# Weight matrices laid out by the host in contiguous 1 MB blocks: a two-layer diffusion backbone on one core

## The chip, the cores and the metric

The kernel runs on one core of a Trainium2 chip. The metric is device time in microseconds of the whole program, inputs in HBM to output in HBM; work of the host before the launch is outside it. A core has a matrix engine (TensorE, in the profile PE for matmuls and PEld for the weight loads that run beside them), VectorE (DVE), ScalarE (ACT), GpSimd (POOL), and SyncE (SP), which here issues every DMA. The transfers are carried out by 16 DMA engines. SBUF is the on-chip memory of 128 partitions, PSUM the memory into which TensorE writes.

## What is computed

Two layers over 512 latent tokens and 256 context tokens of width 1024, all in float32. Layer 0 mixes tokens by pooling, layer 1 by attention with 8 query and 2 key/value heads; each is followed by an MLP of width 4096 with a squared ReLU. Shift, scale and gate of every sub-layer come from a linear map of the conditioning vectors (`w_ada`).

```python
for i in range(DEPTH):
    sh1, sc1, gt1, sh2, sc2, gt2 = ada_mods(c, w_ada[i], b_ada[i])
    csh1, csc1, cgt1, csh2, csc2, cgt2 = ada_mods(c_ctx, w_ada[i], b_ada[i])
    h_lat = modulate(rms_norm(x, g_mix_pre[i]), sh1, sc1)
    h_ctx = modulate(rms_norm(ctx, g_mix_pre[i]), csh1, csc1)
    if i % N_MIXERS == 0:
        y_lat = pool_mixer(h_lat, w_pool[j], pool_scale[j])
        y_ctx = None if last else pool_mixer(h_ctx, w_pool[j], pool_scale[j])
    else:
        y_lat, y_ctx = attention_mixer(h_lat, h_ctx, w_qkv[j], g_q[j], g_k[j], w_o[j], not last)
    x = x + gt1 * rms_norm(y_lat, g_mix_post[i])
    m_lat = sq_relu_mlp(modulate(rms_norm(x, g_mlp_pre[i]), sh2, sc2), w_mlp_in[i], w_mlp_out[i])
    x = x + gt2 * rms_norm(m_lat, g_mlp_post[i])
    if not last:
        ...
```

## The kernel before

**Numbers.** A float32 operand of the large matmuls is split into a high part in float32r and the rest, and a product is made as three matmuls (high by high, high by low, low by high). The splits of the weights are done on the chip, from a raw tile: ScalarE casts the high part (line 126), VectorE subtracts (line 129).

**Loads.** Every weight comes by `raw_load` (line 104): one DMA from SP into a tile `raw` of 128 partitions by 2048 floats, 1 MB. What a partition receives is several rows of the matrix, one per k, cut to the width of the piece: 8 rows of 256 floats (1 KB each) for `w_mlp_in`, `w_pool` and most of `w_ada`; 4 rows of 512 floats (2 KB) for `w_qkv`, `w_o` and the wide pieces of `w_ada` (`w` = 4 in `ada_mm`); 2 rows of 1024 floats (4 KB) for `w_mlp_out`. There are 123 such loads: 48 of `w_ada` (12 with 2 KB rows), 32 of `w_mlp_in`, 32 of `w_mlp_out`, 6 of `w_qkv`, 4 of `w_o`, 1 of `w_pool`. Raw tiles rotate through a pool of four (`rawe`, the start alone) and one of three (`rawp`); a load waits on SP until the former user of its buffer is done, and the loads behind it in SP's program wait with it.

**Stages.** Times are those of the profiled execution. *Start, 0 to 105 us:* the tokens come in and are normalised (lines 325 to 332); the conditioning maps of layer 0 are computed on TensorE, one piece at a time (`ada_mm`, line 225: matmuls of a raw tile with the conditioning columns `cond` into PSUM tile `psada`; VectorE transposes the result, line 227; `ada_sel`, line 232, brings it into columns; VectorE adds the bias into `mods`, line 243). Pooling means are matmuls with a band matrix (line 420, PSUM tile `psm`), and `centred` (lines 452 to 456) modulates them as soon as shift and scale are there. The pooling weights are scaled (line 469) and split, the pooling matmuls (line 480, `pspool`) follow, then norms, gates and the modulation for the MLP (lines 378 to 395). The order of this stage is a table of due times (`Steps`), by which the instructions are written in the program; each engine works off its own list in that order. *First MLP, 105 to about 590 us:* sixteen groups of 256 hidden units, with products of quarter matrices (`weights_sums`, lines 635 to 663; `Seven`, line 677) and output matmuls (line 773, `pso`). VectorE computes the remaining conditioning maps beside it (`ada_sum`, lines 257 to 273). *Projection and attention, about 620 to 860 us* (lines 1020, 1195 to 1237), with `w_qkv` and `w_o` in 2 KB rows. *Second MLP, from about 860 us* (lines 553 and 877), to the output.

Of the kernel before, what the change touches and what calls it, by code (L numbers as in the profile page):

```python
# [17 lines left out]
P = 128  # L18
D = 1024
# [7 lines left out]
NG = FF // 256  # L27
# [5 lines left out]
BW = P + 2 * HALO  # L33
SEGS = ((0, LAT), (LAT, CTX))
SH1, SC1, GT1, SH2, SC2, GT2 = range(6)


TC_OPTS = dict(schedule_with_timeline_sim=True)
# [15 lines left out]
def backbone(ctx: ExitStack, tc, x, c, ctx_in, c_ctx, w_ada, b_ada, g_mix_pre, g_mix_post,  # L54
# [3 lines left out]
    sy, ve, sc, gp, te = nc.sync, nc.vector, nc.scalar, nc.gpsimd, nc.tensor  # L58
# [3 lines left out]
    rawp = ctx.enter_context(tc.tile_pool(name="rawp", bufs=3, side="right"))  # L62
# [17 lines left out]
    cols = const.tile([P, 128], F32, name="cols")  # L80
# [21 lines left out]
    hL = ra[:, KT * TOK:].rearrange("p (k n) -> p k n", n=TOK)  # L102
    accv = acc.rearrange("p (t n) -> p t n", n=D)

    def raw_load(src, width, pool=None):
        t = (pool or pools[0]).tile([P, 2048], F32, tag="raw", name="raw")
        d = sy.dma_start(t.rearrange("p (a b) -> p a b", b=width), src)
        if pinned[0]:
            tc.keep_in_program_order(d)
        return t  # L110
# [24 lines left out]
    class Ring:  # L135
# [1 line left out]
            self.slots, self.n, self.halves = slots, 0, halves  # L137

        def load(self, src, width, pin=False, wait=None):
            raw = raw_load(src, width, rawp)  # L140
# [73 lines left out]
    rowsd, parts, seeded, stale = {}, {}, {}, [0]  # L214

    def ada_mm(i, m, j, w=2):
        src = w_ada[i, :, m * D + j * 256: m * D + j * 256 + w * P].rearrange("(k p) n -> p k n", p=P)
        ps = psB.tile([P, 512], F32, tag="b", name="psada")
        kn = 2048 // (w * P)
        for z in range(KT // kn):  # L220
            raw = raw_load(src[:, kn * z:kn * z + kn], w * P).rearrange("p (k n) -> p k n", n=w * P)
            for k in range(kn):
                at = kn * z + k
                q = 32 * (at % 4)
                te.matmul(ps[q:q + 32, 0:w * P], cond[:, at, :], raw[:, k, :], start=(at < 4), stop=(at >= 4))  # L225
        rows = raw[:, 0, :] if w > 2 else small.tile([P, 256], F32, tag="rows", name="rows", bufs=3)
        ve.transpose(rows, ps[:, 0:w * P])
        rowsd[i, m, j] = ps, rows, w
# [26 lines left out]
                                    op0=ALU.add, op1=ALU.mult)  # L255

    def ada_sum(i, m, j, nc_, part):
        raw = raw_load(w_ada[i, :, m * D + j * 256: m * D + (j + 1) * 256]
                       .rearrange("(k p) n -> p k n", p=P), 256).rearrange("p (k n) -> p k n", n=256)
        rows = []  # L260
        for c in range(nc_):
            r = small.tile([P, 256], F32, tag="rows", name="rows", bufs=3)
            z = ve.tensor_scalar(out=r, in0=raw[:, 0, :], scalar1=cond[:, 0, c:c + 1], scalar2=None, op0=ALU.mult)
# [198 lines left out]
    pw = []  # L462

    def pool_weights():
        wraw = raw_load(w_pool[0].rearrange("g (k p) n -> p (g k) n", p=P), 256)
        pscale = rawp.tile([P, 2048], F32, tag="raw", name="pscale")[:, 0:D]
        sy.dma_start(pscale, pool_scale[0].partition_broadcast(P))
        w4 = wraw.rearrange("p (g k n) -> p g k n", k=2, n=256)
        ve.tensor_tensor(out=w4, in0=w4, in1=pscale.rearrange("p (g n) -> p g n", n=256).unsqueeze(2)
                         .broadcast_to([P, 4, 2, 256]), op=ALU.mult)  # L470
        pw.append((wraw, wpH, wpL))
# [161 lines left out]
            put(3, j, a11, a21, ALU.subtract)  # L633

    def weights_sums(g):
        raw = raw_load(w_mlp_in[0, :, g * 256:(g + 1) * 256].rearrange("(k p) n -> p k n", p=P), 256)
        rv = raw.rearrange("p (k h n) -> p h k n", h=2, n=P)
        b11, b12, b21, b22 = (rv[:, h, 4 * u:4 * u + 4] for u in range(2) for h in range(2))
        k4 = lambda z: z.rearrange("p (k n) -> p k n", n=P)
# [77 lines left out]
    landing = ((21, SC1, 0, 4), (26.3, SH1, 0, 4), (29, SC1, 2, 2), (32, SH1, 2, 2), (39, SC1, 3, 2), (42, SH1, 3, 2),  # L717
               (47.3, GT1, 0, 4), (52.6, GT1, 2, 4), (61, SC2, 0, 4), (66, SH2, 0, 4),
               (69, SC2, 2, 2), (72, SH2, 2, 2), (74.8, SC2, 3, 2), (77.7, SH2, 3, 2))
    for z, m, j, w in landing:  # L720
# [15 lines left out]
    for n, t in enumerate(order):  # L736
        b = 55 + 3 * n
# [88 lines left out]
    def mlp1(inner, last):  # L826
# [5 lines left out]
        pool = closing.enter_context(tc.tile_pool(name="pairs", bufs=1, side="right"))  # L832
# [25 lines left out]
            return w  # L858

        def rows_of(g):  # L860
            r = raw_load(w_mlp_out[1, g * 256:(g + 1) * 256, :].rearrange("(k p) n -> p k n", p=P), D)
            r = h2(r)
            return r[:, :, 0:512], r[:, :, 512:1024]

# [58 lines left out]
        wo_ = []  # L923
        for q in range(2):
            hi, lo = whole(2 * q)
            raw = raw_load(w_mlp_out[1, (NG - 2 + q) * 256:(NG - 1 + q) * 256, :].rearrange("(k p) n -> p k n", p=P), D)
# [243 lines left out]
    aring = Ring([ra[:, 8192:12288], unit[0], unit[1], unit[2]])  # L1170

    def wo_unit(ch, kk, wait=None):
        return aring.load(w_o[0, 512 * kk:512 * kk + 512, 512 * ch:512 * ch + 512]
                          .rearrange("(k p) n -> p k n", p=P), 512, True, wait)

    steps = [(h, t) for h in range(NQ) for t in range(NL)]
    smx = {}
# [163 lines left out]
        "w_pool", "pool_scale", "w_qkv", "g_q", "g_k", "w_o", "w_mlp_in", "w_mlp_out"]  # L1341


def _rope_tables():
    half = HD // 2
    t = np.arange(LAT)
# [45 lines left out]
```

## Time and profile before

| | us |
|---|---|
| three runs | 1179.66, 1181.38, 1181.9 |
| median of the runs | 1181.38 |
| profiled execution, span from first to last instruction | 1177.7 |
| median less span | 3.7 |
| TensorE matmul busy in the span | 1142.0 |
| VectorE, ScalarE, GpSimd busy | 941.6, 638.0, 67.4 |
| moved by DMA | 147.84 MB |

The profile is of one execution; of this execution it gives the span, and no separate time. TensorE's matmuls are pipelined, so that its busy time is an upper reading. An "idle before" in brackets behind a row of the timeline names what ended the engine's wait. For DMA, the share is the mean busy share of the 16 engines, which can read some per cent over 1 when packets overlap, and "to landing" is from the issue on SP to the last byte.

### The profile page before, as it was taken

To read this page: it belongs to the slowest core of one execution; us is meant where nothing else is said; L and a number is where in the kernel's file an instruction comes from. 1 tells how busy PE (TensorE), PEld (TensorE's weight loads), DVE (VectorE), ACT (ScalarE), POOL (GpSimd) and SP (SyncE) were. 2 spreads that over 40 slices of the span, in tenths; PEclk is the share of its full clock that TensorE was granted. 3 is DMA by queue.
4 is the path that set the end of the run, shared out by engine and by line. 5 is a ranking of instruction groups with operands and counts; after the bars stand their busy time and mean duration, and the time that the engine had idled before them with its cause. 6 is when DMAs were issued, how large, how long until landed. Compare 5 with 4: busy or idle time off the path is not lost.

```text
span 1177.7 us, 15984 instructions
## 1 busy us (share of the span) xinstructions
PE 1142.0 (97%) x6170; PEld 988.8 (84%) x6170; DVE 941.6 (80%) x1546; ACT 638.0 (54%) x1087; POOL 67.4 (6%) x120
## 2 busy tenths in 40 slices
PE   5899999999999999999999999999899999999997
PEld 4579888989889988998887889998888888888886
DVE  3786778998988999896787689887686779778876
ACT  3766654555354445555676377862676446435522
POOL 2030000000000000000141210001100000000001
PEclk9899999999999999999999999999999999999999
DMA  9994223444444344344422100115334124314312
GB/s 335 353 310 183 72 72 107 143 143 144 143 143 143 116 136 143 107 133 153 180 72 77 68 1 36 37 42 186 122 116 162 67 94 143 107 36 144 107 39 104
DMA packets 100010, 147.84 MB, mean 126 GB/s; under 512 B 2736, under 2 KB 75872, under 8 KB 99936
## 3 DMA queue, kind: packets, MB, share of 16 engines
q1 hardware_dynamic: 99936, 146.84, 36.6%
q8 instruction: 48, 0.79, 0.3%
q14 instruction: 26, 0.21, 0.1%
HBM read 139.49 MB, written 7.34 MB: 125 GB/s over the span
## 4 chain that ended last, share of the span: by engine, by line
PE 52%; issue 33%; DVE 6%; ACT 4%; POOL 3%; DMA 2%; SPq 0%; POOLq 0%; DVEq 0%; ACTq 0%
PE pso L773 22%; PE psin L677 18%; PE psin L553 3%; PE po L1234 2%; PE psq L1020 2%; PE pss L1195 2%; POOL rs L169 1%; PE psada L225 1%; PE psm L420 1%; POOL rs L1029 1%; ACT junk L154 1%; DVE sm L1199 1%; PE pspt L1220 1%; DVE rows L268 1%; DVE units L1223 1%
## 5 line engine op out<-in xcount | busy, mean ns | idle before, releaser
L773 PE MATMUL pso<-units,rb 128*128 128x512 f32 x1152 | 278.9, 392 | 0.0
L773 PEld LDWEIGHTS pso<-units,rb 128*128 128x128 f32 x1152 | 214.7, 188 | 41.1
L268 DVE SCALAR_TENSOR_TENSOR rows<-raw,cond,rows 128x256 f32<-128x256 f32 x280 | 127.3, 480 | 2.0
L785 DVE TENSOR_TENSOR acc<-acc,pso 128x512 f32<-128x512 f32 x129 | 85.4, 677 | 39.4 <-PE pso L773 39.3
L553 PE MATMUL psin<-ra,rb 128*128 128x512 f32 (+1 forms) x432 | 104.8, 342 | 2.4 <-ACT ra L363 1.6
L877 PE MATMUL pso<-units,pairs 128*128 128x512 f32 x336 | 82.3, 389 | 0.0
L553 PEld LDWEIGHTS psin<-ra,rb 128*128 128x128 f32 x432 | 70.3, 189 | 13.6 <-ACT ra L363 1.9
L553 PE MATMUL psin<-ra 128*128 128x512 f32 x256 | 80.4, 389 | 0.0
L877 PEld LDWEIGHTS pso<-units,pairs 128*128 128x128 f32 x336 | 63.1, 188 | 13.1
L881 DVE TENSOR_TENSOR acc<-acc,pso 128x512 f32<-128x512 f32 x72 | 48.7, 683 | 26.4 <-PE pso L877 26.4
L167 POOL TENSOR_SCALAR ms<-ss 128x1 f32<-128x1 f32 x20 | 9.6, 482 | 1000.2 <-ACT junk L154 988.4
L677 PE MATMUL psin<-ra,units 128*128 128x384 f32 x336 | 65.5, 337 | 0.4 <-ACT psin L689 0.4
L677 PE MATMUL psin<-sums,units 128*128 128x384 f32 x336 | 64.0, 336 | 0.0
L677 PEld LDWEIGHTS psin<-ra,units 128*128 128x128 f32 x336 | 59.8, 188 | 3.9 <-ACT psin L689 0.5
L129 DVE TENSOR_TENSOR units<-raw,units 128x1024 fp32r<-128x1024 f32 (+2 forms) x49 | 55.2, 1154 | 6.5 <-ACT units L126 6.3
L677 PEld LDWEIGHTS psin<-sums,units 128*128 128x128 f32 x336 | 58.9, 188 | 1.6
L126 ACT CAST units<-raw 128x1024 fp32r<-128x1024 f32 (+2 forms) x49 | 46.9, 995 | 17.7 <-PE pso L773 13.7
L553 PEld LDWEIGHTS psin<-ra 128*128 128x128 f32 x256 | 48.1, 188 | 10.0
L553 PE MATMUL psin<-rb 128*128 128x512 f32 (+1 forms) x144 | 52.8, 367 | 0.2 <-DVE rb L364 0.2
L1020 PE MATMUL psq<-units,ra 128*128 128x512 f32 x216 | 51.7, 392 | 0.0
L783 ACT COPY acc<-pso 128x512 f32<-128x512 f32 x48 | 27.1, 586 | 43.6 <-PE pso L773 42.9
L553 PE MATMUL psin<-rb,ra 128*128 128x512 f32 x128 | 49.8, 389 | 0.0
(255 smaller groups left out, 2356.0 us busy)
## 6 DMA issues: line engine op xcount, KB each, us to landing
raw<-in_w_ada SPq DMA_DIRECT2D x48, 1024.0 KB, 5.4
raw<-in_w_mlp_in SPq DMA_DIRECT2D x32, 1024.0 KB, 5.4
raw<-in_w_mlp_out SPq DMA_DIRECT2D x32, 1024.0 KB, 5.1
raw<-in_w_qkv SPq DMA_DIRECT2D x6, 1024.0 KB, 5.2
spill<-xr SPq DMA_DIRECT2D x10, 512.0 KB, 9.1
xr<-spill SPq DMA_DIRECT2D x10, 512.0 KB, 6.6
raw<-in_w_o SPq DMA_DIRECT2D x4, 1024.0 KB, 4.9
xr<-in_x SPq DMA_DIRECT2D x4, 512.0 KB, 4.2
```

Of the source, the lines that this page charges most:

```text
L126: a = sc.copy(hi, raw)
L129: b = ve.tensor_tensor(out=lo, in0=raw, in1=hi, op=ALU.subtract)
L268: ve.scalar_tensor_tensor(out=r, in0=raw[:, k, :], scalar=cond[:, k, c:c + 1], in1=r, op0=ALU.mult, op1=ALU.add)
L553: te.matmul(ps[:, bank, o:o + ln], w[:, k, fs], rhs, start=start, stop=(k == KT - 1 and n == 2), skip_group_check=len(ks) < KT)
L677: te.matmul(bank, w[k], a[k], start=start and k == 0 and m == 0, stop=stop and k == 3 and m == 2, skip_group_check=True)
L773: te.matmul(pss[h][:, 0:cols[h][1]], a[:, f, ts_], w[:, f, cols[h][0]:sum(cols[h])], start=(n == 0 and not seeded[t]), stop=(n == len(seq) ...
L783: sc.copy(d, ps)
L785: ve.tensor_tensor(out=d, in0=d, in1=ps[:, 0:w], op=ALU.add)
L877: te.matmul(ps, a, w, start=(m == 0), stop=(m == len(seq) - 1))
L881: ve.tensor_tensor(out=M[n][:, t], in0=M[n][:, t], in1=ps, op=ALU.add)
L1020: te.matmul(ps, a[:, k, sl], w[:, k % 4, :], start=(k == 0 and n == 0), stop=(k == KT - 1 and n == 2))
L1195: te.matmul(ps[:, c2, 0:384], a[:, sl], b[:, kv, 384 * c2:384 * c2 + 384], start=(n == 0), stop=(n == 2))
```

## The change

The host rearranges every weight matrix before the launch. A block of 1 MB, what one raw tile holds, becomes one contiguous piece of HBM: for each of the 128 partitions one row of 2048 floats (8 KB), in the order in which the tile holds them. The loads name a whole block (`w_mlp_in[i, g]` and so on) and no longer a strided cut of the matrix. The pieces of `w_ada` that are used at width 512 are packed at that width; the table `CONDITIONING` now lists them for both the host and the kernel, and the due times beside it keep their values. Tile shapes, the layout inside a raw tile, the number of loads and their place in the program stay.

```diff
+CONDITIONING = ((SC1, 0, 4), (SH1, 0, 4), (SC1, 2, 2), (SH1, 2, 2), (SC1, 3, 2), (SH1, 3, 2),
+                (GT1, 0, 4), (GT1, 2, 4), (SC2, 0, 4), (SH2, 0, 4), (SC2, 2, 2), (SH2, 2, 2), (SC2, 3, 2), (SH2, 3, 2))
...
-    def raw_load(src, width, pool=None):
+    def raw_load(src, pool=None):
         t = (pool or pools[0]).tile([P, 2048], F32, tag="raw", name="raw")
-        d = sy.dma_start(t.rearrange("p (a b) -> p a b", b=width), src)
+        d = sy.dma_start(t, src)
...
     def ada_mm(i, m, j, w=2):
-        src = w_ada[i, :, m * D + j * 256: m * D + j * 256 + w * P].rearrange("(k p) n -> p k n", p=P)
         ps = psB.tile([P, 512], F32, tag="b", name="psada")
         kn = 2048 // (w * P)
         for z in range(KT // kn):
-            raw = raw_load(src[:, kn * z:kn * z + kn], w * P).rearrange("p (k n) -> p k n", n=w * P)
+            raw = raw_load(w_ada[i, m, j + z]).rearrange("p (k n) -> p k n", n=w * P)
...
-        raw = raw_load(w_ada[i, :, m * D + j * 256: m * D + (j + 1) * 256]
-                       .rearrange("(k p) n -> p k n", p=P), 256).rearrange("p (k n) -> p k n", n=256)
+        raw = raw_load(w_ada[i, m, j]).rearrange("p (k n) -> p k n", n=256)
...
-        wraw = raw_load(w_pool[0].rearrange("g (k p) n -> p (g k) n", p=P), 256)
+        wraw = raw_load(w_pool)
...
-        return rg.load(w_mlp_in[i, :, g * 256:(g + 1) * 256].rearrange("(k p) n -> p k n", p=P), 256, pin, wait)
+        return rg.load(w_mlp_in[i, g], 256, pin, wait)
...
-        return rg.load(w_mlp_out[i, g * 256:(g + 1) * 256, :].rearrange("(k p) n -> p k n", p=P), D, pin)
+        return rg.load(w_mlp_out[i, g], D, pin)
...
-            qring[0].load(w_qkv[0, 512 * kk:512 * kk + 512, 512 * ch:512 * ch + 512]
-                      .rearrange("(k p) n -> p k n", p=P), 512, pin, wait))
+            qring[0].load(w_qkv[ch, kk], 512, pin, wait))
...
+def _blocks(w, width):
+
+    k = 2048 // width
+    rows, cols = w.shape
+    a = w.reshape(rows // (k * P), k, P, cols // width, width).transpose(3, 0, 2, 1, 4)
+    return a.reshape(cols // width, rows // (k * P), P, 2048)
+
+
+def _packed(inputs):
+    out = {n: np.ascontiguousarray(inputs[n]) for n in _INS}
+    ada = np.empty((2, 6, 4, P, 2048), np.float32)
+    for i in range(2):
+        for m in range(6):
+            w = out["w_ada"][i, :, m * D:(m + 1) * D]
+            ada[i, m] = _blocks(w, 256)[:, 0]
+            for n, j, wide in CONDITIONING:
+                if (i, n, wide) == (0, m, 4):
+                    ada[i, m, j:j + 2] = _blocks(w, 512)[j // 2]
...
-    arrays = {f"in_{n}": np.ascontiguousarray(inputs[n]) for n in _INS}
+    arrays = _packed(inputs)
```

Only SP's list reads differently, and there only the shapes of the loads. This is its piece in the start, from the last token tile to the two weight blocks of the first MLP (raw tiles from the weights named behind the arrow, `xr` the tokens, `spill` their copy in HBM), before:

```order
13 L189 DMA xr<-in_ctx 128x1024
14 L107 DMA raw<-in_w_ada 128x4x512 x4
15 L973 DMA grow<-in_g_q 128x128
16 L974 DMA grow<-in_g_k 128x128
17 L467 DMA pscale<-in_pool_scale 128x1024
18 L107 DMA raw<-in_w_ada 128x8x256 x2
19 L107 DMA raw<-in_w_pool 128x8x256
20 L107 DMA raw<-in_w_ada 128x8x256 x2
21 L107 DMA raw<-in_w_ada 128x4x512 x4
22 L107 DMA raw<-in_w_mlp_in 128x8x256
23 L107 DMA raw<-in_w_ada 128x4x512 x4
24 L107 DMA raw<-in_w_ada 128x8x256 x4
```

And the same piece with the change:

```order
13 L191 DMA xr<-in_ctx 128x1024
14 L109 DMA raw<-in_w_ada 128x2048 x4
15 L971 DMA grow<-in_g_q 128x128
16 L972 DMA grow<-in_g_k 128x128
17 L467 DMA pscale<-in_pool_scale 128x1024
18 L109 DMA raw<-in_w_ada 128x2048 x2
19 L109 DMA raw<-in_w_pool 128x2048
20 L109 DMA raw<-in_w_ada 128x2048 x6
21 L109 DMA raw<-in_w_mlp_in 128x2048
22 L109 DMA raw<-in_w_ada 128x2048 x8
```

The loads stand in the same sequence, each in place of its predecessor; two groups merge in the list because their shapes are now alike. The lists of the other engines are the same row by row but for line numbers.

More of the change, by code (lines that the diff above doesn't have):

```diff
@@ L139, in load @@
         def load(self, src, width, pin=False, wait=None):
-            raw = raw_load(src, width, rawp)
+            raw = raw_load(src, rawp)
             s = self.slots[self.n % len(self.slots)]
@@ L635, in weights_sums @@
     def weights_sums(g):
-        raw = raw_load(w_mlp_in[0, :, g * 256:(g + 1) * 256].rearrange("(k p) n -> p k n", p=P), 256)
+        raw = raw_load(w_mlp_in[0, g])
         rv = raw.rearrange("p (k h n) -> p h k n", h=2, n=P)
@@ L716, in backbone @@
         st.at([5.159, 8.462, 12.185, 11.882, 11.6, 13.1][t], rows_b, t)
[L717 to L720, printed above, removed]
+    landing = (21, 26.3, 29, 32, 39, 42, 47.3, 52.6, 61, 66, 69, 72, 74.8, 77.7)
+    for z, (m, j, w) in zip(landing, CONDITIONING):
         ada_at(st, z, 0, m, j, w)
@@ L860, in rows_of @@
         def rows_of(g):
-            r = raw_load(w_mlp_out[1, g * 256:(g + 1) * 256, :].rearrange("(k p) n -> p k n", p=P), D)
+            r = raw_load(w_mlp_out[1, g])
             r = h2(r)
@@ L925, in mlp1 @@
             hi, lo = whole(2 * q)
-            raw = raw_load(w_mlp_out[1, (NG - 2 + q) * 256:(NG - 1 + q) * 256, :].rearrange("(k p) n -> p k n", p=P), D)
+            raw = raw_load(w_mlp_out[1, NG - 2 + q])
             raw = raw.rearrange("p (f n) -> p f n", f=2)
@@ L1172, in wo_unit @@
     def wo_unit(ch, kk, wait=None):
-        return aring.load(w_o[0, 512 * kk:512 * kk + 512, 512 * ch:512 * ch + 512]
-                          .rearrange("(k p) n -> p k n", p=P), 512, True, wait)
+        return aring.load(w_o[ch, kk], 512, True, wait)
     steps = [(h, t) for h in range(NQ) for t in range(NL)]
@@ L1341 @@
         "w_pool", "pool_scale", "w_qkv", "g_q", "g_k", "w_o", "w_mlp_in", "w_mlp_out"]
+def _blocks(w, width):
[13 more added lines that the diff above has]
+                    ada[i, m, j:j + 2] = _blocks(w, 512)[j // 2]
+    out["w_ada"] = ada
+    out["w_pool"] = _blocks(out["w_pool"][0].reshape(D, 256), 256)[0, 0]
+    out["w_mlp_in"] = np.stack([_blocks(w, 256)[:, 0] for w in out["w_mlp_in"]])
+    out["w_mlp_out"] = np.stack([_blocks(w, D)[0] for w in out["w_mlp_out"]])
+    for n in ("w_qkv", "w_o"):
+        out[n] = _blocks(out[n][0], 512)
+    return {f"in_{n}": np.ascontiguousarray(a) for n, a in out.items()}
 def _rope_tables():
```

## The prediction

> **What bounds the kernel now.** I began with the page's head and its 40 slices, to see which engine fills the span and where the transfers fill it.
>
> ```profile
> span 1177.7 us, 15984 instructions
> PE 1142.0 (97%) x6170; PEld 988.8 (84%) x6170; DVE 941.6 (80%) x1546; ACT 638.0 (54%) x1087; POOL 67.4 (6%) x120
> PEclk9899999999999999999999999999999999999999
> DMA  9994223444444344344422100115334124314312
> ```
>
> A slice is 29.4 us. TensorE is busy for 97% of the span; the DMA engines are full only in the first three slices and four to five tenths busy at most after the fourth. So a faster transfer can show itself in the first 100 us, or nowhere. The busy times by stretch say what is left after that:
>
> ```profile
> core 0: us, PE busy (x) PEld busy (x) DVE busy (x) ACT busy (x) POOL busy (x), PEclk, DMA share, GB/s
> 105.00:590.00 485.00, 484.54 (x2470) 435.60 (x2471) 413.47 (x729) 252.29 (x379) 5.98 (x10) 1.00 0.39 128
> 620.00:700.00 80.00, 77.58 (x380) 64.43 (x379) 60.31 (x111) 42.67 (x127) 15.71 (x26) 1.00 0.15 53
> 700.00:760.00 60.00, 57.47 (x426) 55.50 (x425) 56.43 (x116) 49.90 (x110) 0.00 (x0) 1.00 0.11 36
> 900.00:1000.00 100.00, 100.00 (x449) 82.57 (x448) 79.02 (x95) 48.23 (x59) 0.00 (x0) 1.00 0.32 104
> ```
>
> In the first layer's MLP (105 to 590 us) TensorE is idle for 0.46 us of 485, in the second's (the row from 900) for nothing. What it loses between 620 and 760, in projection and attention, falls where the DMA engines are 11 to 15% busy. Next came the list of waits, which says who waits for a transfer at all:
>
> ```profile
> PE pp L206 <- DMA work<-in_g_mlp_post: 6.5, 1, 6.5
> ACT units L643 <- DMA raw<-in_w_mlp_in: 17.8, 11, 6.3
> ACT rb L126 <- DMA raw<-in_w_mlp_in: 4.6, 3, 2.1
> DVE rows L263 <- DMA raw<-in_w_ada: 4.3, 4, 2.1
> ACT ra L126 <- DMA raw<-in_w_mlp_in: 3.0, 5, 1.0
> PEld psada L225 <- DMA raw<-in_w_ada: 0.2, 1, 0.2
> ```
>
> TensorE's one long wait for a transfer (6.5 us) is for a small vector in the first microseconds, which the change does not touch. For a weight load, its weight-load side waits once, 0.2 us. ScalarE and VectorE do wait for weights, 29.7 us over the four rows of theirs, but nearly all of it where TensorE, as the stretches show, never runs dry behind them.
>
> **The change, part by part.** Host work is outside the time. In the kernel 123 loads of 1 MB keep their bytes, order, buffers and waits; only the rows that they name in HBM change: 128 rows of 8 KB each, where 69 loads had 1024 rows of 1 KB, 22 had 512 of 2 KB and 32 had 256 of 4 KB. No operation of a compute engine is added, removed or moved, and the layout inside a raw tile stays.
>
> The price of a load comes from stretches where the queue held one kind of row; the first two lines are SP's issues of them (start, duration), the last three the stretches:
>
> ```profile
> 7.99 4.24 SPq L107 DMA_DIRECT2D raw<-in_w_ada  x4
> 79.15 7.38 SPq L599 DMA_DIRECT2D spill<-xr  x6
> ...
> 16.00:22.00 6.00, 5.05 (x27) 2.93 (x27) 1.60 (x3) 1.07 (x2) 0.32 (x1) 0.72 1.05 387
> 30.00:40.00 10.00, 8.13 (x63) 6.80 (x64) 8.30 (x15) 6.17 (x11) 0.00 (x0) 0.66 1.07 344
> 90.00:95.00 5.00, 5.00 (x49) 4.24 (x48) 4.19 (x10) 4.05 (x8) 0.00 (x0) 1.00 1.03 419
> ```
>
> From 16 to 22 us the first four conditioning loads arrive (2 KB rows), from 30 to 40 loads with 1 KB rows, from 90 to 95 spill stores with 4 KB rows, all with the DMA share at 1 and the moved GB/s in the last column. A load is 1.049 MB, so it costs 2.71 us in 2 KB rows, 3.05 us in 1 KB rows, 2.50 us in 4 KB rows. No row shows 8 KB. Halving the rows saved 0.34 us and then 0.21 us, so the next halving should save about 0.1: I take 2.4 us (estimate from the three rows). The bound on the good side is that value, since the gains halve; on the bad side stands the nearest row with larger packets:
>
> ```profile
> q1 hardware_dynamic: 99936, 146.84, 36.6%
> q8 instruction: 48, 0.79, 0.3%
> ```
>
> The 48 packets of queue q8 carry 16 KB each; 0.3% of 16 engines' span is 56.5 us, 1.18 us a packet, or 222 GB/s over 16 engines, which would make a load 4.7 us. These packets go one at a time and to other memory, the three load rows get faster with every doubling, so I stay at 2.4 and keep 4.7 for a rival. So a load gains 0.65 us where its rows were 1 KB, 0.3 us at 2 KB, 0.1 us at 4 KB.
>
> [...]
>
> Now what these gains are worth, at the places where a reader stands nearest behind its load. The loads' own line gives the issue (duration in ns, start) and the time from issue to landing, the timeline the reader:
>
> ```profile
> L107 SPq DMA_DIRECT2D raw<-in_w_ada x21: 367/368/3965, 8.0 to 119.9; - x21
> ...
> L107 SPq DMA_DIRECT2D raw<-in_w_ada x1: 379/379/379, 20.2 to 20.2; - x1
> DMA to landing us min/median/max: 8.2/8.2/8.2
> ...
> L107 SPq DMA_DIRECT2D raw<-in_w_ada x1: 3965/3965/3965, 29.7 to 29.7; - x1
> DMA to landing us min/median/max: 12.8/12.8/12.8
> ```
>
> ```profile
> 28.34 0.13 DVE L243 TENSOR_TENSOR mods<-psada,cols 128x8 f32<-128x8 f32 x1
> 28.47 0.16 PEld L232 LDWEIGHTS psada<-raw,sel 128*32 128x32 f32 x8 [0.89 <-DVE mods L243]
> 28.59 1.07 PE L225 MATMUL psada<-raw,cond 128*32 128x256 f32 x16
> 31.87 3.14 PE L420 MATMUL psm<-gate,acc 128*128 128x136 f32 x12 [2.20 <-DVE work L454]
> 42.69 0.59 PEld L225 LDWEIGHTS psada<-raw,cond 128*32 128x32 f32 x16 [1.21 <-ACT work L452]
> 48.84 0.16 PEld L225 LDWEIGHTS psada<-raw,cond 128*32 128x32 f32 x8 [0.24 <-DMA raw<-in_w_ada]
> 49.84 2.90 PE L480 MATMUL pspool<-rb,ra 128*128 128x256 f32 x22
> ```
>
> The fifth conditioning load lands at 20.2 + 8.2 = 28.4 us, its matmuls start at 28.59; but ahead of them in TensorE's program stand the selection matmuls at 28.47, released by VectorE's addition at 28.34. The load could come 2 us earlier and nothing would start earlier. The load issued at 29.7 lands at 42.5; its matmuls at 42.69 were released by ScalarE (L452), which frees the PSUM buffer. At 48.84 the load itself ends the wait, 0.24 us; the pool matmuls at 49.84 stand behind it and feed the chain. That is the one place with a gain: 0.24 us, bounded by 0 (the pool matmuls waited for VectorE as well) and 0.24.
>
> The back-pressure on SP's queue should shrink: the issue at 29.7 took 3965 ns, where the middle one of 21 takes 368. What SP then issues sooner still waits for a buffer that TensorE or VectorE releases, so I cost this at nothing; the cover is those releases, and if it were gone the loads behind would come up to 3.6 us earlier, to readers who do not wait. Loads of the MLP stages gain 0.1 to 0.65 us for ScalarE and VectorE in the shade of TensorE's full rows. If that cover were gone, the first MLP could gain its 0.46 us of idle time, no more.
>
> Sum against the profiled execution: 1177.7 - 0.2 = 1177.5 us of span. The median of the runs, 1181.38, is 3.7 us above the span, for launch and end, which stay: **1181.2 us**, no change within what a measurement of this kernel can tell (0.2%, 2.4 us).
>
> **Rivals.** *A: the start is bound by the transfers after all.* Between 8 and 66 us twelve loads with 2 KB rows and six with 1 KB rows pass, with the DMA engines full; if the whole start moved up with them, it would gain 12 x 0.3 + 6 x 0.65 = 7.5 us: 1173.9 us. For it: the full DMA slices, and readers a few tenths behind their loads at three places above. Against it: the releaser at two of the three is another engine, and 0.2 us is the whole wait.
>
> *B: 8 KB rows are slower.* The place is the same start, whose readers have no slack: with each load at 4.7 us instead of 2.85 on the mean, fourteen loads up to the first MLP's weights come 14 x 1.85 = 26 us late, and TensorE behind them: 1207 us. It decides from about 2.9 us a load (360 GB/s) on; at 3.5 us it would cost some 9 us. For it: the instruction queue's packets. Against it: three load rows with the opposite trend.
>
> *C: the clock of the start falls otherwise.*
>
> ```profile
> 17.41:20.82 3.41, 3.41 (x15) 1.50 (x15) 0.85 (x2) 1.07 (x2) 0.00 (x0) 0.50 1.05 386
> 27.65:31.06 3.41, 1.22 (x28) 0.59 (x24) 1.91 (x7) 2.01 (x3) 0.00 (x0) 1.00 0.90 294
> 31.06:34.48 3.42, 2.61 (x11) 2.61 (x12) 3.13 (x7) 3.42 (x8) 0.00 (x0) 0.50 1.02 316
> 34.48:37.89 3.41, 3.41 (x31) 2.23 (x30) 3.06 (x8) 1.69 (x3) 0.00 (x0) 0.50 1.10 359
> ```
>
> TensorE was granted half its clock from 17.4 to 20.8 and from 31.1 to 37.9 us, the latter after a stretch of 3.41 us in which it was busy for 1.22. Its 9.4 us of work in these three stretches would take 4.7 at the full clock. If a load that comes earlier filled the idle stretch, up to 4.7 us would be won (1176.7 us); if an idle moment elsewhere drew two more half-clock stretches, 6.8 us of work would take 3.4 us longer (1184.8 us). Against the gain: the idle stretch at 28 to 31 us ends with a wait of 2.20 us for VectorE (the row at 31.87 above), not for a load. [...]
>
> *D: the descriptors are cut back to 4 KB or less on the way*, so the change does half of what it says; the time is the forecast's.
>
> **How the numbers follow.** Forecast 0.68, A 0.12 (one of the three readers above is released by its load, so a part of A is likelier than the whole), B 0.06, C 0.05 on the fast side and 0.04 on the slow side, D 0.05. Faster by over 0.2%: A and fast C, 0.17. Within: forecast and D, 0.73. Slower: B and slow C, 0.10. The forecast's own range is 1179.0 to 1183.0, the runs' spread (1179.66 to 1181.9) widened by half a microsecond or so. Taking in a part of A and of both sides of C down to 1177.5 and up to 1183.5 leaves out about 0.19.
>
> **What would show it.** The rows to look at first are the loads' own:
>
> ```profile
> raw<-in_w_mlp_in SPq DMA_DIRECT2D x32, 1024.0 KB, 5.4
> ```
>
> Right: over 400 GB/s or idle DMA engines from 30 to 40 us of the changed profile; `w_mlp_in` loads that land in about 4.8 us after the issue instead of 5.4; gaps in front of SP's loads in place of long issues; yet the pool matmuls at 49.6 to 49.8 us and TensorE full from 105 us on, as now; packets in DMA queue q1 down from 99936 to some 25,600, since 123 x 128 rows stand for 90,112. Wrong: the timeline's marks at 28.6, 42.7 and 49.8 us moved by over 1 us (A, or B if later), other half-clock stretches (C), or a packet count near 41,000 (D). A TensorE that is idle for a microsecond or more between 105 and 590 us would upset the whole argument.

## The result and the profile after

| | before | after |
|---|---|---|
| median of 13 runs each, us | 1180.11 (1179.02 to 1182.22) | 1180.54 (1178.71 to 1182.91) |
| ratio after to before, 95% interval | | 1.0000 (0.9991 to 1.0009) |
| span of the profiled execution, us | 1177.7 | 1178.7 |

The change makes no difference that can be measured; a gain or a loss of more than 1.1 us is excluded by the interval. Two slow executions are left out of the ratios of this document: one of 1910 us, of the experiment with 1 KB rows, and one of 4029 us, of the kernel before beside it. The loads, though, did get faster. From the page of the changed kernel come its head, the main queue and the median time of the loads from issue to landing:

```profile
span 1178.7 us, 15984 instructions
PE 1142.6 (97%) x6170; PEld 989.5 (84%) x6170; DVE 941.9 (80%) x1546; ACT 637.5 (54%) x1087; POOL 67.2 (6%) x120
q1 hardware_dynamic: 25568, 146.84, 34.1%
...
raw<-in_w_mlp_in SPq DMA_DIRECT2D x32, 1024.0 KB, 4.8
raw<-in_w_mlp_out SPq DMA_DIRECT2D x32, 1024.0 KB, 5.0
```

As many instructions, busy times within 1 us of those before, a quarter of the packets (25,568 for 99,936), and `w_mlp_in` lands in 4.8 us instead of 5.4. In the busy times by stretch the last column is GB/s and the one ahead of it the share of the DMA engines:

```profile
16.00:22.00 6.00, 5.30 (x20) 3.07 (x21) 1.83 (x4) 1.24 (x4) 0.79 (x2) 1.00 1.01 427
30.00:40.00 10.00, 7.79 (x63) 5.94 (x53) 8.09 (x17) 7.12 (x12) 0.00 (x0) 0.66 1.00 411
105.00:590.00 485.00, 484.23 (x2467) 435.24 (x2468) 413.61 (x730) 251.84 (x379) 5.86 (x10) 1.00 0.36 128
```

Where the queue holds nothing but loads it now moves 427 and 411 GB/s (387 and 344 before): 2.46 and 2.55 us for 1.049 MB. The last row shows why that is worth nothing later on: in the first MLP the DMA share fell from 0.39 to 0.36, and TensorE is idle for 0.77 us of 485, where it was idle for 0.46. The waits for weights tell the same (total, times, longest):

```profile
ACT units L643 <- DMA raw<-in_w_mlp_in: 11.5, 4, 5.6
ACT ra L128 <- DMA raw<-in_w_mlp_in: 2.9, 3, 2.0
DVE rows L263 <- DMA raw<-in_w_ada: 2.3, 3, 1.3
ACT junk L156 <- DMA xr<-in_ctx: 1.6, 1, 1.6
ACT rb L128 <- DMA raw<-in_w_mlp_in: 1.1, 1, 1.1
```

The four rows of weights add up to 17.8 us, 29.7 before. Twelve microseconds of waiting went away on ScalarE and VectorE without one of them reaching TensorE. Its own wait for `w_ada`, 0.2 us before, is not there (nor is it in a second profile of the kernel before, as shown below). The row for `xr<-in_ctx`, a token tile that the change does not touch, has grown: ScalarE waits 1.6 us for it, where it waited 0.3.

The start, in the timeline (start, duration, engine, operation; idle before and its releaser in brackets):

```profile
16.28 1.27 PE L420 MATMUL psm<-gate,acc 128*128 128x136 f32 x4 [2.19 <-DVE acc L332]
...
25.88 2.78 PE L226 MATMUL psada<-raw,cond 128*32 128x512 f32 x24
...
29.37 0.13 DVE L244 TENSOR_TENSOR mods<-psada,cols 128x8 f32<-128x8 f32 x1
...
29.62 1.07 PE L226 MATMUL psada<-raw,cond 128*32 128x256 f32 x16
...
32.90 3.14 PE L420 MATMUL psm<-gate,acc 128*128 128x136 f32 x12 [2.21 <-DVE work L454]
...
43.73 1.07 PE L226 MATMUL psada<-raw,cond 128*32 128x256 f32 x16 [0.73 <-ACT work L452]
...
49.44 0.38 PE L480 MATMUL pspool<-rb,ra 128*128 128x256 f32 x1
49.75 0.16 PEld L226 LDWEIGHTS psada<-raw,cond 128*32 128x32 f32 x8
...
50.75 2.88 PE L480 MATMUL pspool<-rb,ra 128*128 128x256 f32 x22
```

Against the rows of before, 28.59, 31.87 and 42.69 us have become 29.62, 32.90 and 43.73. Each stands 1.03 or 1.04 us later, and the same difference, about a microsecond, is still there at the end of the two spans. So between these two profiles the start neither gained nor lost anything behind 20 us; what differs lies ahead of it. TensorE's wait at 16.28 is for VectorE's normalised token tile. In the profile of before the same place stands at 15.48 and has waited 1.20 us, not 2.19: here is most of the microsecond. Whether the change or chance put it there was the first question for experiments.

### The profile page after: what moved, and what is told of

It reads as the page before. It is cut to its first block, busy times and chain, and to the rows that moved or that the text cites. A ratio compares the mean times of both kernels' runs of the same rounds, so it can differ in the third digit from the quotient of the medians.

```text
span 1178.7 us, 15984 instructions
## 1 busy us (share of the span) xinstructions
PE 1142.6 (97%) x6170; PEld 989.5 (84%) x6170; DVE 941.9 (80%) x1546; ACT 637.5 (54%) x1087; POOL 67.2 (6%) x120
## 2 busy tenths in 40 slices
DMA packets 25642, 147.84 MB, mean 125 GB/s; under 512 B 2736, under 2 KB 5216, under 8 KB 9824
## 3 DMA queue, kind: packets, MB, share of 16 engines
q1 hardware_dynamic: 25568, 146.84, 34.1%
## 4 chain that ended last, share of the span: by engine, by line
PE 54%; issue 33%; DVE 5%; ACT 3%; POOL 3%; DMA 1%; SPq 0%; POOLq 0%; DVEq 0%; ACTq 0%
PE pso L771 22%; PE psin L677 18%; PE psin L553 3%; PE po L1230 2%; PE psy L1256 2%; PE psq L1018 2%; PE pss L1191 2%; POOL rs L171 1%; PE psada L226 1%; PE psm L420 1%; POOL rs L1027 1%; ACT junk L156 1%; DVE sm L1195 1%; PE pspt L1216 1%; DVE units L1219 1%
## 5 line engine op out<-in xcount | busy, mean ns | idle before, releaser
L553 PEld LDWEIGHTS psin<-ra,rb 128*128 128x128 f32 x432 | 70.3, 189 | 13.7 <-ACT ra L363 1.9
L879 DVE TENSOR_TENSOR acc<-acc,pso 128x512 f32<-128x512 f32 x72 | 48.8, 683 | 28.6 <-PE pso L875 28.6
L128 ACT CAST units<-raw 128x1024 fp32r<-128x1024 f32 (+2 forms) x49 | 46.9, 995 | 17.7 <-PE pso L771 13.7
L553 PE MATMUL psin<-rb,ra 128*128 128x512 f32 x128 | 49.8, 389 | 0.0
```

The source lines that it names most:

```text
L128: a = sc.copy(hi, raw)
L553: te.matmul(ps[:, bank, o:o + ln], w[:, k, fs], rhs, start=start, stop=(k == KT - 1 and n == 2), skip_group_check=len(ks) < KT)
L879: ve.tensor_tensor(out=M[n][:, t], in0=M[n][:, t], in1=ps, op=ALU.add)
```

## Experiments

**Theories.** The prediction's own, with its threshold: the loads of the start come as early as their readers need them, up to about 2.9 us a load, and beyond that each tenth costs. Rival A: the start is bound by the transfers, and a load's time counts in full. Beside them stood the microsecond at 16 us, then the question whether the written order, and not the transfers, keeps the earlier landings from being used. Where the kernel before ran beside an experiment, its median was 1181.27 us (7 runs, with the first four experiments), 1179.41 (22 runs, the next four) and 1179.72 (33 runs, the last four). Ratios are to these.

### The microsecond at the start

Three single runs: the kernel before again, the changed kernel again, and the changed kernel with its first four conditioning loads in 2 KB rows.

> The kernel before once more, for a second profile. In the two profiles so far the changed kernel runs 1.0 us behind from 17 us on (18 us, where the last context tile has been normalised) and stays there. Theory N (noise of one execution): the last context tile's landing, 12.9 us in the first profile of before and 13.7 us in that of the change, scatters by some 0.7 us among executions of one kernel, so that the second profile of before can lie anywhere from 1177 to 1179.5 us. Theory L (large rows crowd the last token tiles): before lands again at 12.9 us and spans 1177.5 to 1178 us.

> The changed kernel once more. Theory L: last context tile at 13.5 us or later again, the 4 KB packets beside 8 KB packets at about 206 ns instead of 167 ns, span 1178.5 us or more. Theory N: landing anywhere from 12.7 to 13.8 us, span 1177 to 1179.5 us. Both: the timeline from 20 us on has the same distances between its marks as in the first profiles, to 0.3 us.

> The changed kernel, but the first four conditioning loads, the ones right behind the token tiles, in 2 KB rows again. Theory L: the last context tile lands at 12.9 us as before, the span falls back by 0.7 to 1.0 us to about 1177.7 us. Theory N: no link, 1177 to 1179.5 us whatever the landing of the first loads.

The third differs from the changed kernel in the rows of four blocks, which the host packs accordingly:

```diff
+def row_of(name, block):
+    return 512 if name == "in_w_ada" and block in (0, 1, 4, 5) else 2048
...
-        d = sy.dma_start(t, src)
+        r = row_of(src.tensor.name, src.offset // (2048 * P))
+        flat = src.rearrange("p n -> (p n)").rearrange("(a p b) -> p a b", p=P, b=r)
+        d = sy.dma_start(t.rearrange("p (a b) -> p a b", b=r), flat)
```

Measured: 1179.96, 1179.82 and 1179.12 us, with spans of 1178.2, 1178.0 and 1177.3. ScalarE takes the first context tile when it has landed, and the first conditioning matmuls of TensorE follow behind that. First before, then before again:

```profile
11.68 1.06 ACT L154 ACTIVATE junk<-xr 128x1024 bf16<-128x1024 f32 x1 [0.33 <-DMA xr<-in_ctx]
...
18.16 1.94 PE L225 MATMUL psada<-raw,cond 128*32 128x512 f32 x8
```

```profile
11.88 1.06 ACT L154 ACTIVATE junk<-xr 128x1024 bf16<-128x1024 f32 x1 [0.99 <-DMA xr<-in_ctx]
...
18.57 1.94 PE L225 MATMUL psada<-raw,cond 128*32 128x512 f32 x8
...
25.86 2.78 PE L225 MATMUL psada<-raw,cond 128*32 128x512 f32 x24
```

And after, then after again:

```profile
12.48 1.06 ACT L156 ACTIVATE junk<-xr 128x1024 bf16<-128x1024 f32 x1 [1.64 <-DMA xr<-in_ctx]
...
19.18 1.94 PE L226 MATMUL psada<-raw,cond 128*32 128x512 f32 x8
```

```profile
11.47 1.06 ACT L156 ACTIVATE junk<-xr 128x1024 bf16<-128x1024 f32 x1 [0.23 <-DMA xr<-in_ctx]
...
18.16 1.94 PE L226 MATMUL psada<-raw,cond 128*32 128x512 f32 x8
...
25.75 2.78 PE L226 MATMUL psada<-raw,cond 128*32 128x512 f32 x24
```

The changed kernel, run again, reaches its first conditioning matmul at 18.16 us, exactly where the kernel before had it, so the microsecond is not the change's. It comes with the landing of the first context tile: ScalarE starts on it at 11.68, 11.88, 12.48 and 11.47 us, and the matmuls that stand at 16.28 in the profile after follow 3.80 us behind that in all four. The expectations named another tile, the last one. Nobody waits for that: it landed at 12.9, 13.5, 13.7 and 13.6 us, and the second profile of the changed kernel, with 13.6, has no delay. The theory that 8 KB rows crowd the tokens falls; the run with four loads in 2 KB rows (18.18 us for the first conditioning matmul) adds nothing to that. What both theories expected, equal distances between the marks from 20 us on to 0.3 us, did not come: the next block of conditioning matmuls follows 6.69 and 6.70 us later in the first two profiles, 7.29 and 7.59 us in the second two. So a mark near 25 us scatters by a microsecond among executions of one kernel, in two ways, and 1 us between two single profiles says nothing of a change.

### How much slower may the loads of the start be?

Same edit, other rows: the loads of the start (20 of `w_ada`, `w_pool`, the first two blocks of `w_mlp_in`, 23 in all; the first expectation says 22) in rows of 512 B, then of 1 KB. The other 100 loads keep 8 KB, and the order of work is that of the changed kernel.

```diff
+def row_of(name, block):
+    return 128 if (name == "in_w_ada" and block < 20) or name == "in_w_pool" or (name == "in_w_mlp_in" and block < 2) else 2048
```

> The changed kernel with the loads of the start (22 of 1 MB: conditioning of layer 0 but its last gate, pooling weights, first two blocks of the first MLP) in rows of 512 B instead of 8 KB; all else alike, and the same order on every engine. By the trend of the rows a load takes about 3.6 us instead of 2.5. Forecast's theory (readers follow their loads by tenths of a us, the engines set the pace as long as a load takes up to about 2.9 us): fourteen loads up to the first MLP's weights are late by 14 x (3.6 - 2.9) = 10 us less what idle moments of the queue take up: 5 to 10 us slower, all of it before 105 us. Rival A (transfers set the pace of the start at any size): 14 x (3.6 - 2.5) = 15 us slower than the changed kernel. Rival S (ample slack): under 1.5 us slower.

Measured: 1191.06 us (1189.52 to 1191.7), ratio 1.0081 (1.0064 to 1.0098). A stretch of the start:

```profile
30.00:40.00 10.00, 5.88 (x44) 4.03 (x48) 6.18 (x14) 7.12 (x12) 0.00 (x0) 0.66 1.02 290
```

and TensorE's waits for conditioning loads:

```profile
PE psada L232 <- DMA raw<-in_w_ada: 5.7, 4, 2.5
PEld psada L232 <- DMA raw<-in_w_ada: 2.2, 3, 1.1
```

290 GB/s is 3.62 us a load, 0.72 above the threshold; for the fourteen loads up to the first MLP's weights the prediction's formula gives 14 x 0.72 = 10 us. The ratio makes it 9.6 (7.6 to 11.6). TensorE now waits some 7 us for them (a wait of 1.1 us for one load stands in both rows), where it waited 0.2 in the kernel before. A price counted from zero slack, 14 x (3.62 - 2.5) = 16 us, is too high.

With 256 in place of 128 (rows of 1 KB):

> The changed kernel with the 23 loads of the start in rows of 1 KB instead of 8 KB (before: eleven of them in 1 KB rows and twelve in 2 KB rows), same order on every engine. A load takes 3.05 us. With 512 B rows (3.7 us a load) TensorE was 9.2 us behind at 64 us. Theory with a threshold (forecast): a slope of fourteen loads per us puts the threshold at 3.7 - 9.2 / 14 = 3.05 us, so 0 to 0.5 us slower than the changed kernel, within 0.1% of both kernels. Rival without threshold (every us of transfer counts, fewer of them on the path): 9.2 x (3.05 - 2.5) / (3.7 - 2.5) = 4 us slower.

The same stretch:

```profile
30.00:40.00 10.00, 7.58 (x82) 5.84 (x83) 8.27 (x21) 7.12 (x12) 0.00 (x0) 0.83 1.08 344
```

Measured: 1181.41 us, ratio 1.0012 (1.0003 to 1.0021), 1.4 us. The formula says 14 x (3.05 - 2.9) = 2.1 us, a count without slack 14 x 0.55 = 8. The expectation had put the threshold at 3.05 us and so 0 to 0.5 us slower, its rival 4 us; the measured 1.4 us (0.4 to 2.5) is between them and nearer the threshold. So the bend lies near 2.9 to 3.0 us a load, just above what the loads of before took on the mean (2.85): the kernel before stood at the edge of its slack, on the good side.

### Half the bytes

Each of the 20 conditioning loads of layer 0's start brings half its block, and the matmuls use that half twice; the other half of these weights is left out.

```diff
-        d = sy.dma_start(t, src)
+        d = sy.dma_start(t[:, 0:n], src[:, 0:n])
...
-            raw = raw_load(w_ada[i, m, j + z]).rearrange("p (k n) -> p k n", n=w * P)
+            cut = True
+            raw = raw_load(w_ada[i, m, j + z], n=1024 if cut else 2048).rearrange("p (k n) -> p k n", n=w * P)
...
-                te.matmul(ps[q:q + 32, 0:w * P], cond[:, at, :], raw[:, k, :], start=(at < 4), stop=(at >= 4))
+                te.matmul(ps[q:q + 32, 0:w * P], cond[:, at, :], raw[:, k % (1024 // (w * P)) if cut else k, :], start=(at < 4), stop=(at >= 4))
```

> The changed kernel, but each of the twenty conditioning loads of layer 0 in the start brings half of its block, and the matmuls use the half that is there twice: as many matmuls on the same shapes, 10 MB less to move before 85 us. The output is not the reference's. The scheduler puts some 80 rows of TensorE's list elsewhere. Theory with a threshold: transfers are not what the start waits for at 2.5 us a load, and not at 1.25; within 1.5 us of the changed kernel, the rest being the other order. Rival A and the rival without threshold: twenty loads shorter by 1.25 us bring 8 to 15 us.

Measured: 1175.48 us (1173.38 to 1176.53), ratio 0.9963 (0.9949 to 0.9977): 4.4 us faster. Both expectations missed it, the threshold theory (1.5 us at most) on the low side. The timeline shows what was bought:

```profile
15.86 1.07 PE L227 MATMUL psada<-raw,cond 128*32 128x512 f32 x8
...
25.32 0.26 DVE L245 TENSOR_TENSOR mods<-psada,cols 128x8 f32<-128x8 f32 x2 [2.49 <-PE psada L234]
...
46.46 2.89 PE L481 MATMUL pspool<-rb,ra 128*128 128x256 f32 x22
```

The conditioning matmuls stand earlier in TensorE's list, between the pooling means; about 80 rows of that list are placed otherwise. A planner writes the order out when the kernel is built. What it reckons with is not shown: rows of 1, 2 and 8 KB got the same lists, but in two later runs rows of 512 B alone moved instructions. The modulation vectors `mods` are there at 25.3 us, 4.05 before the changed kernel's 29.37, and the pooling matmuls follow at 46.46, 4.3 before its 50.75. In the changed kernel three blocks of conditioning matmuls stand together at 25.88, behind the pooling means, though the last of their loads has landed at 23.7:

```profile
L109 SPq DMA_DIRECT2D raw<-in_w_ada x4: 328/431/647, 8.2 to 10.0; - x4
DMA to landing us min/median/max: 8.0/10.8/13.7
```

(issued at 10.0, 13.7 us to the landing.) So there is time to be had at the start, but by order and bytes together, and TensorE's pace has a part in it: the first eight conditioning matmuls take 1.07 us here (at 15.86) and 1.94 us in the changed kernel (at 19.18), as long as in the kernel before at a granted clock of 0.50 (at 18.16). This run does not part the three.

### Another order, in both layouts

The load of the pooling weights and their scaling on VectorE (line 469) are moved ahead of conditioning work by their due times, once a little, once more, each with the new and the old layout. The lists of the compute engines are alike in the two layouts.

```diff
-    st.at(33.5, pool_weights)
-    st.at(36.5, lambda: split(*pw[0]))
+    st.at(30.2, pool_weights)
+    st.at(33.0, lambda: split(*pw[0]))
```

> The changed kernel with the due time of the pooling weights moved from 33.5 to 30.2 (their split from 36.5 to 33.0): on SP their load goes ahead of one conditioning load, on VectorE their scaling (L469) stands one operation after the conditioning additions of 34.7 us instead of six. About 15 rows on TensorE and VectorE change places with it. Order theory: the earlier landings gained nothing because the written order, made for the old landings, had no reader for them; a reader that stands earlier uses them: the scaling starts 1 to 2 us earlier than 38.8, and the time falls 1 to 3 us below the changed kernel (1177.5 to 1179.5 where that has 1180.5). Rival, compute pace: TensorE and VectorE set the pace of the start whatever lands when, and the conditioning matmuls pushed back lose what the pool gains: within 1 us.

> The same two due times in the kernel before; the compute engines' lists are those of the run with the changed layout, row by row. Order theory: here the loads land 1 to 2.5 us later at this place (36.5 against 35.2 for the pool, 42.5 against 40.2 for the last narrow conditioning load), so this order gains 1 us or more less than in the new layout, perhaps nothing at all: 1179 to 1182. Rival, compute pace: the same time as with the new layout, within 0.5 us.

And with 28.3 and 31.5 as due times:

> The changed kernel with the pooling weights due at 28.3 (split 31.5): their load goes ahead of two conditioning loads, the scaling stands right behind the first two centring operations on VectorE. Order theory: the block lands near 30 us and the scaling runs near 33 us, the narrow conditioning matmuls come 2.5 us later each; gain of 0 to 3 us over the changed kernel, and the new layout is ahead of the old one in this order by 1 us or more. Rival, compute pace: within 1 us of the changed kernel, and the layouts alike within 0.5 us.

> The same in the kernel before, the compute engines' lists again those of the run with the new layout. Order theory: the scaling waits for a load of 3.05 us a block, and the conditioning loads behind it come 0.5 us a block later than in the new layout: 1 to 3 us slower than the run with the new layout. Rival, compute pace: alike within 0.5 us.

| due at | new layout, us | ratio | old layout, us | ratio |
|---|---|---|---|---|
| 30.2 | 1180.34 | 0.9996 (0.9987 to 1.0005) | 1180.67 | 1.0004 (0.9995 to 1.0012) |
| 28.3 | 1179.31 | 0.9995 (0.9987 to 1.0004) | 1180.94 | 1.0004 (0.9996 to 1.0013) |

No order is measurably faster, in either layout. The scaling and the pooling matmuls in the changed kernel as run again, with 30.2, and with 28.3:

```profile
38.20 2.28 DVE L469 TENSOR_TENSOR raw<-raw,pscale 128x2048 f32<-128x2048 f32 x1
...
50.17 2.68 PEld L480 LDWEIGHTS pspool<-rb,ra 128*128 128x128 f32 x22 [0.84 <-DVE work L454]
```

```profile
34.29 2.28 DVE L469 TENSOR_TENSOR raw<-raw,pscale 128x2048 f32<-128x2048 f32 x1
...
50.36 2.69 PEld L480 LDWEIGHTS pspool<-rb,ra 128*128 128x128 f32 x22 [0.84 <-DVE work L454]
```

```profile
29.18 2.29 DVE L469 TENSOR_TENSOR raw<-raw,pscale 128x2048 f32<-128x2048 f32 x1
...
49.44 2.21 PEld L480 LDWEIGHTS pspool<-rb,ra 128*128 128x128 f32 x18 [0.84 <-issue]
```

The scaling starts 4 and 9 us earlier; the block of pooling matmuls starts 0.2 us later and 0.7 us earlier, no more than such marks scatter. In the first two of the three its releaser is VectorE's line 454, which modulates pooled tokens with `mods`. In the third a conditioning load is now waited for, just ahead of the block, since its reader comes earlier and the load does not; first with the new layout, then with the old:

```profile
48.44 0.16 PEld L226 LDWEIGHTS psada<-raw,cond 128*32 128x32 f32 x8 [1.24 <-DMA raw<-in_w_ada]
```

```profile
49.43 0.16 PEld L225 LDWEIGHTS psada<-raw,cond 128*32 128x32 f32 x8 [2.31 <-DMA raw<-in_w_ada]
```

So the weights' side of pooling can be moved by 9 us without a gain over the written order: what it gains is spent on TensorE's wait for a conditioning load. The order theory's gain did not come. Its other half, a new layout that is ahead by 1 us or more, came with 28.3: from the single pooling matmul to the block (46.74 to 49.44 us with the new layout, 46.65 to 50.43 with the old) lie 1.1 us less, and the first MLP's main work begins 1.0 us earlier (104.44 and 105.42 us). Taken directly, the two groups of eleven runs differ by 1.6 us in the mean, with 0.8 to 2.4 us as a 95% interval; the rival's 0.5 us lies outside. With 30.2 the groups differ by 0.4 us (-0.4 to 1.2), nothing that shows, though TensorE there waits 1.3 us for conditioning loads with the new layout and 4.2 us with the old. A half-clock stretch at 847 us fell into two of the four profiled executions (below); how often it fell into the other runs is not known, so how much of the 1.6 us is the layout's stays open beyond the 1.0 us that the two profiles show at the start.

### The later loads

All 32 loads of `w_mlp_out` in 512 B rows, the rest in 8 KB; a handful of instructions change places.

```diff
+def row_of(name, block):
+    return 128 if name == "in_w_mlp_out" else 2048
```

> The changed kernel with the 32 loads of the second MLP matrices (w_mlp_out) in rows of 512 B: 3.7 us a load instead of 2.5. The order differs in a handful of rows. Forecast's theory (from 105 us on TensorE's own work hides every transfer): within 1.2 us of the changed kernel. Rival (later transfers are on the path as well): up to 32 x 1.2 = 38 us slower.

The page's line for these loads (its size column counts one row, the last column is the median time to landing), and the first MLP's stretch:

```profile
raw<-in_w_mlp_out SPq DMA_DIRECT2D x32, 0.5 KB, 6.6
```

```profile
105.00:590.00 485.00, 484.30 (x2467) 435.34 (x2468) 413.50 (x729) 251.62 (x379) 5.99 (x10) 1.00 0.39 128
```

Measured: 1179.69 us, ratio 1.0003 (0.9994 to 1.0013). Each load lands 1.6 us later (6.6 for 5.0) and TensorE in the first MLP does not notice (busy for 484.30 us of 485, 484.23 in the changed kernel). Then all 100 loads that the start does not use:

```diff
+def row_of(name, block):
+    return 2048 if (name == "in_w_ada" and block < 20) or name == "in_w_pool" or (name == "in_w_mlp_in" and block < 2) else 128
```

> The changed kernel with all 100 loads behind the start in rows of 512 B, 3.7 us a load instead of 2.5; the scheduler orders some 70 rows of TensorE's list and 170 of VectorE's otherwise. Forecast's theory: the DMA engines would be busy for some 55% instead of 36% of the first MLP, still hidden: within 3 us of the changed kernel, the other order included. Rival (later transfers are on the path): 100 x 1.2 = 120 us slower at full price, over 10 us if a tenth of it counts.

The first MLP's stretch and the longest of the waits for weights:

```profile
105.00:590.00 485.00, 482.34 (x2447) 431.06 (x2446) 410.17 (x722) 248.71 (x375) 3.97 (x6) 1.00 0.46 128
```

```profile
ACT units L649 <- DMA raw<-in_w_mlp_in: 50.9, 12, 12.0
```

Measured: 1186.52 us (1185.67 to 1187.8), ratio 1.0058 (1.0044 to 1.0072), some 7 us, more than the 3 expected. TensorE is idle for 2.66 us of the first MLP instead of 0.77, and ScalarE waits 50.9 us for weights. The cover of the later loads is large, not endless: 100 loads at some 1.1 us more each (3.6 for 2.5) would be 110 us in full, and 7 came out. Some 70 rows of TensorE's list and more of VectorE's change places in this kernel, so a part of the 7 us may be the order's.

## Why the prediction was right, and where it was not

**The result** lies 0.7 us from the predicted 1181.2, as "no change". That it lies so near is luck in part: the prediction started from a median of 1181.38 us of three runs, the thirteen have 1180.11, and runs of one kernel spread over 3 to 4 us.

**The price of a load** held: 2.46 to 2.55 us against the estimate of 2.4. The gains did fall with every doubling of the rows (3.05, 2.71, 2.50 us), but the last doubling brought nothing that shows (the 4 KB figure is from `spill`, which are stores and not loads). `w_mlp_in` landed after 4.8 us, as forecast. From 1 KB to 8 KB rows a load fell by 0.50 to 0.59 us.

**The one gain, 0.24 us at 48.84**, did not come from the change. In the changed profile 1.31 us lie between the single pooling matmul and the block of 22 (49.44 to 50.75), where 1.42 lay (48.42 to 49.84). But the kernel before, run again, has no such wait either, and the same 1.31 us:

```profile
48.98 0.38 PE L480 MATMUL pspool<-rb,ra 128*128 128x256 f32 x1
...
50.29 2.41 PE L480 MATMUL pspool<-rb,ra 128*128 128x256 f32 x18
```

The load is waited for in one execution and not in the next; of the bounds, 0 and 0.24, the lower one is what the runs show.

**The threshold of 2.9 us a load** is borne out by the runs that made the loads slower: it gave 10 and 2.1 us for rows of 512 B and 1 KB, and 9.6 and 1.4 were measured (counted from the 2.85 us of the loads before, as the sum of rival B does, it would be 10.8 and 2.8). It says nothing of what faster loads could bring under another order, which is where it missed.

**Issues on SP.** The one of 3965 ns is gone; the longest load issue up to 60 us takes 647 ns in the changed kernel. As forecast, what SP issues sooner found no reader.

**Rivals.** *A* falls for this change, since 7.5 us are far outside the interval. Its thought, that earlier loads can shorten the start, may hold in another form: half the bytes together with another order gain 4.4 us. So "no reader waits for a load" must not be taken for "the start cannot use earlier loads": the first is a property of the written order. That the layout alone could gain with another order is not shown. *B* falls, as 8 KB rows run at 411 to 427 GB/s; the 16 KB packets that spoke for it carry none of the loads (0.79 MB on q8, beside 146.84 MB on q1). *D* falls by the packet count (25,568, where it expected some 41,000). *C* is real, but not the change's doing. In the changed profile these two stretches of the start have the granted clock in the third column from the right:

```profile
17.41:20.82 3.41, 2.99 (x13) 1.16 (x12) 1.36 (x3) 1.07 (x2) 0.00 (x0) 1.00 1.01 425
32.10:38.93 6.83, 6.03 (x40) 4.85 (x41) 6.21 (x14) 5.09 (x10) 0.00 (x0) 0.50 1.02 429
```

The first row reads as if the half-clock stretch at 17.4 us were gone. The matmuls say that it is not: eight wide conditioning matmuls take 1.94 us in the changed profile (19.18), as they do under the 0.50 of before (18.16), where eight of the same shape take 1.04 us later in the same profile (48.46). The 1.00 of this early row is thus no proof of a full clock. The other stretch lies a microsecond later; nothing was won by it, since TensorE waits for tokens at 16 us and for VectorE at 32.90 anyway. At 847 us TensorE has no such waits (4.50 us busy of 4.50), and a half clock there cost time. With the pooling weights due at 30.2 (new layout) and at 28.3 (old layout) such a stretch fell at that place. The first of these two profiles reads 0.62 for it, as shown here, the second 0.69:

```profile
846.50:851.00 4.50, 4.50 (x28) 4.50 (x27) 3.64 (x4) 2.69 (x2) 0.00 (x0) 0.62 0.00 0
```

Those two spans are 1179.8 and 1179.9 us; their sisters, with a full clock there, have 1177.0 and 1177.4. The same row of matmuls of line 553 takes 7.1 us there (845.66 to 852.76 with the new layout) and 5.6 us in the sisters, so TensorE loses 1.5 us in this stretch, somewhat over half of the difference; the rest, 1.3 and 1.0 us, was there when the first MLP began. The stretch falls in either layout; what sets its place is not shown.

**Marks of the start.** The prediction called a shift of over 1 us at 28.6, 42.7 and 49.8 us a sign of A or B. The marks moved by 1.03, 1.04 and 0.91, and it was neither. The kernel before, run again, has the block of conditioning matmuls at 25.86 us, where its first profile had 24.85: 0.41 us of that came ahead of the first conditioning matmul, 0.60 behind it. A mark in one profile has to be read against the one ahead of it and against a second profile of the same kernel.

**Left open:** whether the conditioning matmuls of the start, put where the 8 KB loads land (18.6, 21.1, 23.7 us) instead of 25.88, would gain a part of the 4.4 us. It was not tried.

## What to carry to other kernels

Here, in the order as it stood, a faster transfer was worth no more than what its nearest reader on TensorE waited for it (0.24 us at the most, and a ratio of 1.0000 came out); list the releasers of the matmuls behind the loads before a layout is rewritten, and look for the load time from which they begin to wait. That time is found by making the loads slower on purpose, in two sizes. If a kernel's order is written or planned ahead, a faster load may need a new order too. Moving the pooling weights here only brought TensorE to wait for a conditioning load instead (1.24 us with the new layout, 2.31 us with the old); the readers that head the chain, those of `mods`, are the ones to try next.

## What the runs showed of the hardware

- The 512 B rows did not cross as 512 B packets. With 23 loads in 512 B rows the page of that run counts 34,400 packets on q1; the other 25,568 - 23 x 128 = 22,624 taken off, 11,776 are left, 512 a load, so a packet carries 2 KB, four rows. With 1 KB rows it is a packet a row: the page of the kernel before counts 75,872 packets under 2 KB, that of the changed kernel 5,216, and the 70,656 between them are 1024 for each of 69 loads. Yet the 512 B rows moved 290 GB/s, where 1 KB rows moved 344: the packet count alone did not tell the speed.

- SP paid for the 512 B rows at the issue, 3.08 us in the middle of 13 `w_ada` loads of the start (0.33 with 8 KB rows), which is nearly the time of a load:

```profile
L115 SPq DMA_DIRECT2D raw<-in_w_ada x13: 702/3084/3677, 8.1 to 59.3; - x13
```
